# A new order for the second mixer's stage: loads, scores, page keys and page values of a hybrid decoder layer

## The chip, the cores and the metric

The kernel runs on one core of a Trainium2 chip. Its engines work side by side, each through its own list of instructions in order: TensorE (PE in the profile; PEld is its weight load), VectorE (DVE), ScalarE (ACT), GpSimd (POOL) and SyncE (SP), which here only starts transfers. They wait for each other by semaphores. The metric is the time of one execution on the device, in microseconds, as the median of several runs. One further execution is profiled; all views of the trace are of that one.

## The reference

One inference step of one decoder layer, for a prompt of 512 tokens and for 8 single sample tokens, which the kernel carries as N = 520 columns of a transposed activation. The layer adds two token mixers that work on the same normed input, merges them by sigmoid gates, and ends with a gated feed-forward part with a short convolution. Cut to the second mixer, forgetting attention with 8 heads of 128:

```python
q_f = rmsnorm(split_heads(fq, F_HEADS), f_qnorm_w)
k_f = rmsnorm(split_heads(fk, F_HEADS), f_knorm_w)
# prompt: causal, in blocks of 128 queries
s = einsum('bqhd,bkhd->bhqk', qi, k) * scale
s = s + (F_q - F_k)                  # F: running sum of log forget values
s = where(qpos >= kpos, s, -inf)
out = einsum('bhqk,bkhd->bqhd', softmax(s), v)
# sample: one new token over 2 pages of 128 cached keys and values, plus itself
pk = cache_k[layer, page_table]; pv = cache_v[layer, page_table]
merged = sigmoid(ga) * (y_m @ w_proj_a) + sigmoid(gb) * (y_f @ w_proj_b)
```

## The kernel before

Every large product is fp32, made of three products of rounded parts: a weight tile `raw` of 512 KB comes by a transfer of SyncE, ScalarE casts it to `wh` (L167), VectorE makes the rest `wl` (L168), and TensorE multiplies wh and wl with the two parts of the activation. Seven `raw` tiles and three pairs wh, wl exist at a time. A weight tile serves eight blocks of 128 rows; a block is six matmuls of 128x260, and `dense` takes one entry of the list `bg` behind each block. A block with its entry is called a step.

The stage of the second mixer is the last 12 column blocks of the input product (the gates of the merge), 16 steps each, so 192 steps. What runs beside them is written down in `plan`, a table from step to functions, which `put(step, function, ...)` fills. A head has 22 steps (`HP`), its base is b = 1 + 22 x head:

- `f_load` starts five transfers of 260 KB on SyncE: q, the row of inverse roots for q (spread over all partitions), k, the row for k, v. All five have the name `fi`.
- `f_norm` multiplies q and k by weight and row (L1534, two instructions of VectorE) and stores k (GpSimd's queue). `f_split` casts both on ScalarE (`fqh`, `fkh`) and makes the rests on GpSimd (`fql`, `fkl`). `f_forget` spreads the head's forget sums (`nFb`). `f_values` transposes v (`vtp`) and splits it.
- `f_scores(i)`, i from 0 to 3, makes the scores `fS` of a block of queries against all keys up to it, 128 to 512 wide, adds the forget sums and takes the maximum (VectorE L1566), the exponential (ScalarE L1568), and scales by the sum (VectorE L1570). The result is `fs`.
- `f_turn(j)` transposes the weights (`fPT`, L1581) and splits them (`fph`, `fpl`), `f_attend(j)` multiplies them with the values (`fy`), `y_split` splits the result.

The sample tokens run beside it. There are 16 pages of work, two halves of the heads by 8 tokens: `s_load` fetches a token's query row (`qb`, 256 KB, SyncE) and two tiles of cached keys (`kp`, gathers of GpSimd), `s_scores` multiplies and sums them on VectorE. These tiles come from a pool of nine, so three pages fit at a time. Behind the last, `s_bias`, `s_softmax` (transposes `sS`) and `s_weights` (transposes `sPT`, a memset of `pp` by GpSimd, a copy into it) make the weights; `s_gather` fetches 32 tiles of cached values (`vp`, GpSimd), `s_attend(n)` multiplies four of them (`sO`), and `s_heads` transposes each pair of results (`sOT`), which `ob` holds.

Ahead of the stage `run_pairs` works through pairs of column blocks; functions of the table `late_steps` run at its steps, seven to a pair: the inverse roots (`root_load`, `root_make`) and the sample rows (`rows_load`, `rows_make`) at the end. There the order of TensorE, VectorE and ScalarE is that of the program (class `Ordered`). In the stage itself the framework's scheduler orders the instructions of each engine, by the program's order and its own estimate of when operands are there; `plan` says only in which order they come to it.

## Time and profile before

| | |
|---|---|
| median of 3 runs | 2883.55 us (2879.86 to 2886.05) |
| profiled execution | 2878.56 us, span 2876.9 us, mean granted clock .995 |
| busy over the span | PE 2828.8 us (98%), DVE 2157.2 (75%), ACT 1360.1 (47%), POOL 409.3 (14%) |
| the stage | from 1004 to 1236 us |

A row of the timeline has the start in us, the duration, the engine, the line, the operation, output and inputs with their shapes, how many such instructions follow each other, and in brackets the idle time ahead of it and what ended it. A row of the waits has the line that waited, what released it, the total in us, how many times, and the longest. Numbers behind names of buffers are left out there.

### The profile page before, as it was taken

What the parts mean: (1) busy time and instruction counts of PE and PEld (TensorE: products, weight loads), DVE (VectorE), ACT (ScalarE), POOL (GpSimd) and SP (SyncE); (2) the same over time, 40 slices, a digit from 0 to 9 for tenths busy, and PEclk for the clock granted to TensorE, in tenths of its full rate; (3) what the DMA queues carried; (4) which work ended last, traced back from release to release, by engine and by line L of the source; (5) the groups of instructions that cost most, each with busy time, mean ns of one, the idle gap of its engine ahead of it and who ended that gap; (6) DMA issues with size and microseconds to landing.
All of it is one profiled execution on the core that took longest, in us unless ns stands there. A gap on an engine that the chain in (4) does not pass through costs nothing. (4 is left out here: it accounts for less than half of the span.)

```text
span 2876.9 us, 57590 instructions
## 1 busy us (share of the span) xinstructions
PE 2828.8 (98%) x23318; PEld 2715.0 (94%) x23318; DVE 2157.2 (75%) x3318; ACT 1360.1 (47%) x2131; POOL 409.3 (14%) x687
## 2 busy tenths in 40 slices
PE   8999999999999999899999999999999999999999
PEld 6888998999999989699999999999999999999999
DVE  5986755676767767568888887777787788787787
ACT  4335543455455544444555444444444445534543
POOL 0001111211101144501211010111110111100100
PEclk9999999999999999999999999999999999999999
DMA  9946658855555577566682444444444346745753
GB/s 339 311 145 205 216 184 274 278 177 195 180 178 191 179 240 232 196 214 219 206 266 85 129 134 142 144 147 144 143 132 130 115 151 181 213 149 170 191 159 104
DMA packets 226756, 531.44 MB, mean 185 GB/s; under 512 B 30305, under 2 KB 83025, under 8 KB 226489
## 3 DMA queue, kind: packets, MB, share of 16 engines
q1 hardware_dynamic: 187296, 426.89, 45.9%
q0 software_dynamic: 38752, 100.64, 11.5%
q8 instruction: 183, 3.00, 0.4%
q14 instruction: 85, 0.69, 0.1%
q10 hardware_dynamic: 440, 0.23, 0.0%
HBM read 451.28 MB, written 72.92 MB: 182 GB/s over the span
## 5 line engine op out<-in xcount | busy, mean ns | idle before, releaser
L60 DVE TENSOR_TENSOR wl<-raw,wh 128x1024 fp32r<-128x1024 f32 (+1 forms) x666 | 802.1, 1205 | 352.3 <-ACT wh L60 348.5
L60 ACT CAST wh<-raw 128x1024 fp32r<-128x1024 f32 (+1 forms) x666 | 689.4, 1036 | 757.2 <-DVE raw L60 389.1
L60 PE MATMUL x<-bf,wh 128*128 128x260 f32 x2624 | 475.8, 282 | 2.0 <-DVE tg L60 2.0
L60 DVE TENSOR_TENSOR raw<-raw,raw 128x1024 f32<-128x1024 f32 x339 | 413.9, 1221 | 5.8
L60 PEld LDWEIGHTS x<-bf,wh 128*128 128x128 f32 x2624 | 403.2, 188 | 2.2 <-ACT wh L60 2.2
L60 PE MATMUL x<-bf,wl 128*128 128x260 f32 x1312 | 369.7, 282 | 0.0
L60 PEld LDWEIGHTS x<-bf,wl 128*128 128x128 f32 x1312 | 246.8, 188 | 0.0
L60 PE MATMUL y<-bf,wh 128*128 128x260 f32 x1312 | 238.8, 282 | 0.0
L60 PEld LDWEIGHTS y<-bf,wh 128*128 128x128 f32 x1312 | 201.4, 188 | 0.0
L168 DVE TENSOR_TENSOR wl<-raw,wh 128x1024 fp32r<-128x1024 f32 x92 | 113.5, 1235 | 110.5 <-ACT wh L167 106.7
L60 PE MATMUL x<-ff,wh 128*128 128x260 f32 x1024 | 186.2, 283 | 0.0
L60 PE MATMUL x<-hf,wh 128*128 128x260 f32 x1008 | 185.5, 284 | 0.0
L60 PE MATMUL y<-bf,wl 128*128 128x260 f32 x656 | 184.7, 282 | 0.0
L167 ACT CAST wh<-raw 128x1024 fp32r<-128x1024 f32 x92 | 96.4, 1048 | 179.3 <-DMA raw<-in_w_in 40.7
L60 PEld LDWEIGHTS x<-hf,wh 128*128 128x128 f32 x1008 | 155.0, 188 | 13.4 <-issue 6.7
L60 PEld LDWEIGHTS x<-ff,wh 128*128 128x128 f32 x1024 | 157.6, 188 | 0.0
L60 PE MATMUL x<-ff,wl 128*128 128x260 f32 x512 | 144.5, 282 | 0.0
L60 PE MATMUL x<-hf,wl 128*128 128x260 f32 x504 | 142.3, 282 | 0.8 <-DVE wl L60 0.8
L60 PE MATMUL fo<-fe,wh 128*128 128x260 f32 x768 | 125.5, 284 | 1.1 <-DVE fo L60 0.9
L60 PEld LDWEIGHTS y<-bf,wl 128*128 128x128 f32 x656 | 123.7, 188 | 0.0
L60 PE MATMUL z<-bf,wh 128*128 128x260 f32 x656 | 120.6, 284 | 0.0
L60 PEld LDWEIGHTS fo<-fe,wh 128*128 128x128 f32 x768 | 105.8, 188 | 2.5 <-DVE fo L60 2.1
(640 smaller groups left out, 7077.9 us busy)
## 6 DMA issues: line engine op xcount, KB each, us to landing
raw<-in_w_fi SPq DMA_DIRECT2D x176, 512.0 KB
raw<-in_w_in SPq DMA_DIRECT2D x155, 512.0 KB
ar<-in_w_ada SPq DMA_DIRECT2D x192, 256.0 KB
raw<-in_w_ada SPq DMA_DIRECT2D x96, 512.0 KB
raw<-in_w_fo SPq DMA_DIRECT2D x64, 512.0 KB
raw<-in_w_out SPq DMA_DIRECT2D x32, 512.0 KB
raw<-in_w_fo SPq DMA_DIRECT2D x32, 384.0 KB
dff<-cc POOLq DMA_DIRECT2D x44, 260.0 KB
```

The costliest lines, as they stand in the source:

```text
L60: return lambda *a, **k: self.tc.keep_in_program_order(getattr(self.eng, op)(*a, **k))
L167: S.copy(wh[:, :n], raw[:, :n])
L168: V.tensor_tensor(wl[:, :n], raw[:, :n], wh[:, :n].bitcast(F32), op=ALU.subtract)
```

## The change

- `f_load`, `f_norm` and the list of heads are made ahead of `run_pairs`. Head 0's loads run in the last pair, 9 steps behind its start, when one operand of the pairs is given up (`hX.pop(5)`), and its norm 4 steps later, so both are ordered there as the pair's own work is. `rows_make` comes one step sooner.
- The other heads: loads at b - 18 instead of b - 12, `f_values` at b + 3 instead of b + 4 (and the tile of v is free behind it), scores at b + 8, 9, 11, 12 instead of 10, 11, 13, 15, turns as before at b + 20 to b + 22, `f_attend` from b + 26 instead of b + 25.
- Sample tokens: page loads at 6 + 7i instead of 2 + 8i, their scores at 18 + 7i instead of 14 + 8i. Softmax and weights 10 steps sooner (127 and 131), products of the values 8 steps sooner (from 137). The first eight gathers of values come at 126 to 133 instead of the first four at 135 to 138, each further group of four one to four steps behind a product, for the group two ahead (before: four to one steps ahead of a product, for the next group). `s_heads` seven steps behind its product instead of four.

```diff
--- before.py
+++ after.py
@@ -1428,6 +1428,25 @@
     root = {}
     dss, drr = dram([2, FH, N], "dss"), dram([2, FH, N], "drr")
 
+    def f_load(H):
+        H.q, H.k, H.rq, H.rk, H.v = (st("fi") for _ in range(5))
+        for t, src in ((H.q, dqk[0, H.i]), (H.rq, drr[0, H.i].partition_broadcast(P)), (H.k, dqk[1, H.i]),
+                       (H.rk, drr[1, H.i].partition_broadcast(P)), (H.v, dv[H.i])):
+            nc.sync.dma_start(t[:, :N], src)
+
+    def f_norm(H):
+        for t, w, r in ((H.q, qwc, H.rq), (H.k, nkw, H.rk)):
+            V.scalar_tensor_tensor(t[:, :N], t[:, :N], w, r[:, :N], op0=ALU.mult, op1=ALU.mult)
+        G.dma_start(O["kT"][:, H.i, :], H.k[:, :N])
+        H.rq = H.rk = None
+
+    heads = []
+    for hh in range(FH):
+        H = Head()
+        H.i, H.p, H.pt = hh, [], {}
+        heads.append(H)
+    H = None
+
     gates = list(range(NG, KC + NB2))
     others = [GatePair(gates[2 * i:2 * i + 2]) for i in range(len(gates) // 2)]
     others[1:1] = [ValuePair((2 * i, 2 * i + 1)) for i in range(FH // 2)]
@@ -1455,7 +1474,8 @@
         ada_store(SH2, late_ada.pop("sb"))
 
     t0 = 7 * (len(units) - 2)
-    late_steps = {7 * (KC + 2): late_turn, t0 + 1: root_load, t0 + 3: root_make, t0 + 6: rows_load, t0 + 9: rows_make}
+    late_steps = {7 * (KC + 2): late_turn, t0 + 1: root_load, t0 + 3: root_make, t0 + 6: rows_load, t0 + 8: rows_make,
+                  t0 + 9: lambda: (hX.pop(5), f_load(heads[0])), t0 + 13: on(f_norm, heads[0])}
     for k in range(KC):
         late_steps.update({7 * (1 + k) + 3: on(late_load, k), 7 * (1 + k) + 6: on(late_product, k)})
 
@@ -1523,18 +1543,6 @@
     yf = []
     log_exp()
 
-    def f_load(H):
-        H.q, H.k, H.rq, H.rk, H.v = (st("fi") for _ in range(5))
-        for t, src in ((H.q, dqk[0, H.i]), (H.rq, drr[0, H.i].partition_broadcast(P)), (H.k, dqk[1, H.i]),
-                       (H.rk, drr[1, H.i].partition_broadcast(P)), (H.v, dv[H.i])):
-            nc.sync.dma_start(t[:, :N], src)
-
-    def f_norm(H):
-        for t, w, r in ((H.q, qwc, H.rq), (H.k, nkw, H.rk)):
-            V.scalar_tensor_tensor(t[:, :N], t[:, :N], w, r[:, :N], op0=ALU.mult, op1=ALU.mult)
-        G.dma_start(O["kT"][:, H.i, :], H.k[:, :N])
-        H.rq = H.rk = None
-
     def f_split(H):
         H.qr = split(sp, "s", H.q, "fq", SEQ, G)
         H.kr = split(sp, "s", H.k, "fk", SEQ, G)
@@ -1547,6 +1555,7 @@
         H.vt = split(sp, "s", ps, "fv", 3 * P)
         H.last = st("last")
         S.copy(H.last[:, :P], ps[:, 3 * P:])
+        H.v = None
 
     def f_forget(H):
         psb = spread(R["nF"], H.i, "nFb")
@@ -1702,45 +1711,40 @@
         V.tensor_tensor(lo[:, SEQ:N], yS[:, :, hh], hi[:, SEQ:N].bitcast(F32), op=ALU.subtract)
 
     HP = 22
-    heads = []
-    for hh in range(FH):
-        H = Head()
-        H.i, H.p, H.pt = hh, [], {}
-        heads.append(H)
+    for hh, H in enumerate(heads):
         b = 1 + hh * HP
         if hh:
-            put(b - 12, f_load, H)
-        put(b, f_norm, H)
+            put(b - 18, f_load, H)
+            put(b, f_norm, H)
         put(b + 2, f_split, H)
         put(b + 1, f_forget, H)
-        put(b + 4, f_values, H)
-        for s, i in ((10, 0), (11, 1), (13, 2), (15, 3)):
+        put(b + 3, f_values, H)
+        for s, i in ((8, 0), (9, 1), (11, 2), (12, 3)):
             put(b + s, f_scores, H, i)
         for j in range(3):
             put(b + 20 + j, f_turn, H, j)
         for j in range(NB):
-            put(b + 25 + j, f_attend, H, j)
-        put(max(150 + 4 * hh, b + 30), y_split, hh)
-    f_load(heads[0])
+            put(b + 26 + j, f_attend, H, j)
+        put(max(148 + 4 * hh, b + 31), y_split, hh)
     for e in range(2):
         put(0, s_rows, e)
     for i in range(16):
-        put(8 * i + 2, s_load, i)
-        put(14 + 8 * i, s_scores, i)
-    put(136, s_bias)
-    put(137, s_softmax)
-    put(141, s_weights)
-    for i in range(4):
-        put(135 + i, s_gather, i)
+        put(6 + 7 * i, s_load, i)
+        put(18 + 7 * i, s_scores, i)
+    put(126, s_bias)
+    put(127, s_softmax)
+    put(131, s_weights)
+    for i in range(8):
+        put(126 + i, s_gather, i)
     for n in range(8):
-        t = 145 + 5 * n
+        t = 137 + 5 * n
         put(t, s_attend, n)
-        for i in range(n * 4 + 4, min(n * 4 + 8, 32)):
-            put(t - 4 + i % 4, s_gather, i)
+        for i in range(n * 4 + 8, min(n * 4 + 12, 32)):
+            put(t + 1 + i % 4, s_gather, i)
         if n % 2:
-            put(t + 4, s_heads, n // 2)
+            put(t + 7, s_heads, n // 2)
     for hh in range(FH):
-        put(185 if hh < FH - 1 else 187, y_sample, hh)
+        put(183 if hh < FH - 1 else 188, y_sample, hh)
 
     def run(fs):
         for f in fs:
```

How this moves instructions, at three places. First, head 0's softmax, while head 1's loads come. The order of SyncE there, before (`dqk` holds q and k, `drr` the rows of roots, `dv` the values, `dqf` the sample tokens' query rows):

```order
L1615 DMA qb1737_12150<-dqf1720_12094 128x512
L1615 DMA qb1751_12229<-dqf1720_12094 128x512
L1615 DMA qb1776_12353<-dqf1720_12094 128x512
L161 DMA raw1937_13196<-in_w_in 128x1024
L1530 DMA fi1757_12251<-dqk874_5549 128x520
L1530 DMA fi1759_12253<-drr878_5556 128x520
L1530 DMA fi1758_12252<-dqk874_5549 128x520
L1530 DMA fi1760_12254<-drr878_5556 128x520
```

and now:

```order
L1624 DMA qb1750_12203<-dqf1725_12107 128x512
L1435 DMA fi1745_12187<-dqk874_5549 128x520
L1435 DMA fi1747_12189<-drr878_5556 128x520
L1435 DMA fi1746_12188<-dqk874_5549 128x520
L1435 DMA fi1748_12190<-drr878_5556 128x520
L161 DMA raw1946_13226<-in_w_in 128x1024
L1435 DMA fi1749_12191<-dv872_5548 128x520
L1624 DMA qb1768_12303<-dqf1725_12107 128x512
```

Two of the three first query rows went from ahead of head 1's loads to behind them. VectorE, from the maximum of head 0's last scores (the ISA row with `fS`) to their scaling by the sum, before:

```order
L1566 ISA fs1774_12334,sm1775_12335<-fS1773_12329,nfb1736_12148 128x512
L1566 ISA sm1775_12335 128x1
L1570 TENSOR_SCALAR fs1763_12272<-fs1763_12272,sm1764_12273 128x256
L1569 RECIPROCAL sm1767_12297<-sm1767_12297 128x1
L1567 TENSOR_SCALAR sm1775_12335<-sm1775_12335 128x1
L1534 SCALAR_TENSOR_TENSOR fi1758_12252<-fi1758_12252,nkw_5552,fi1760_12254 128x520
L1570 TENSOR_SCALAR fs1766_12296<-fs1766_12296,sm1767_12297 128x384
L60 TENSOR_TENSOR kp1738_12152<-kp1738_12152,qb1737_12150 128x512
L1569 RECIPROCAL sm1775_12335<-sm1775_12335 128x1
L60 TENSOR_REDUCE sc_12095<-kp1738_12152 128x4
L60 TENSOR_TENSOR kp1739_12153<-kp1739_12153,qb1737_12150 128x512
L1570 TENSOR_SCALAR fs1774_12334<-fs1774_12334,sm1775_12335 128x512
```

and now:

```order
L1575 ISA fs1766_12296,sm1767_12297<-fS1765_12291,nfb1736_12148 128x512
L1575 ISA sm1767_12297 128x1
L1578 RECIPROCAL sm1764_12279<-sm1764_12279 128x1
L1439 SCALAR_TENSOR_TENSOR fi1746_12188<-fi1746_12188,nkw_5552,fi1748_12190 128x520
L1579 TENSOR_SCALAR fs1763_12278<-fs1763_12278,sm1764_12279 128x384
L168 TENSOR_TENSOR wl1818_12545<-raw1816_12542,wh1817_12544 128x1024
L1576 TENSOR_SCALAR sm1767_12297<-sm1767_12297 128x1
L60 TENSOR_TENSOR kp1769_12305<-kp1769_12305,qb1768_12303 128x512
L60 TENSOR_REDUCE sc_12108<-kp1769_12305 128x4
L1578 RECIPROCAL sm1767_12297<-sm1767_12297 128x1
L60 TENSOR_TENSOR kp1770_12306<-kp1770_12306,qb1768_12303 128x512
L1579 TENSOR_SCALAR fs1766_12296<-fs1766_12296,sm1767_12297 128x512
```

The page that is multiplied there was the first (its query row is the first that SyncE fetched) and is now the second, whose query row stands last in SyncE's rows above; a weight row `wl` is there as well. TensorE took the transposes of head 0's first three `fs`, then the fourth behind 12 gate matmuls; now it takes the four one behind the other.

Second, head 4's softmax on VectorE, before, from three rows behind the maximum of the last scores to their scaling:

```order
L1569 RECIPROCAL sm1994_13485<-sm1994_13485 128x1
L1567 TENSOR_SCALAR sm2003_13543<-sm2003_13543 128x1
L1534 SCALAR_TENSOR_TENSOR fi1987_13463<-fi1987_13463,qwc_5550,fi1989_13465 128x520
L1570 TENSOR_SCALAR fs1993_13484<-fs1993_13484,sm1994_13485 128x256
L1569 RECIPROCAL sm1997_13509<-sm1997_13509 128x1
L1534 SCALAR_TENSOR_TENSOR fi1988_13464<-fi1988_13464,nkw_5552,fi1990_13466 128x520
L1570 TENSOR_SCALAR fs1996_13508<-fs1996_13508,sm1997_13509 128x384
L60 TENSOR_TENSOR kp1964_13343<-kp1964_13343,qb1963_13341 128x512
L1569 RECIPROCAL sm2003_13543<-sm2003_13543 128x1
L60 TENSOR_REDUCE sc_12095<-kp1964_13343 128x4
L60 TENSOR_TENSOR kp1965_13344<-kp1965_13344,qb1963_13341 128x512
L1570 TENSOR_SCALAR fs2002_13542<-fs2002_13542,sm2003_13543 128x512
```

and now, from that maximum itself:

```order
L1575 ISA fs2002_13524,sm2003_13525<-fS2001_13519,nfb1965_13349 128x512
L1575 ISA sm2003_13525 128x1
L1578 RECIPROCAL sm2000_13507<-sm2000_13507 128x1
L1576 TENSOR_SCALAR sm2003_13525<-sm2003_13525 128x1
L1579 TENSOR_SCALAR fs1999_13506<-fs1999_13506,sm2000_13507 128x384
L1578 RECIPROCAL sm2003_13525<-sm2003_13525 128x1
L1579 TENSOR_SCALAR fs2002_13524<-fs2002_13524,sm2003_13525 128x512
```

The norm of head 5 and a page of keys stood in it and no longer do.

Third, GpSimd at the first group of cached values, before (`fql` and `fkl` are head 6's):

```order
L225 TENSOR_TENSOR fql2076_13950<-fi2042_13762,fqh2075_13949 128x512
L225 TENSOR_TENSOR fkl2078_13954<-fi2043_13763,fkh2077_13953 128x512
L868 DMA vp2079_13957<-in_cache_v,idx0_2452 128x512
L868 DMA vp2084_13976<-in_cache_v,idx0_2452 128x512
L868 DMA vp2092_14010<-in_cache_v,idx0_2452 128x512
L868 DMA vp2093_14021<-in_cache_v,idx0_2452 128x512
L1654 MEMSET pp1721_12096 128x512
L868 DMA vp2120_14148<-in_cache_v,idx1_2456 128x512
```

and now (`dsg` is a store of a gate):

```order
L868 DMA vp2059_13853<-in_cache_v,idx0_2452 128x512
L868 DMA vp2063_13873<-in_cache_v,idx0_2452 128x512
L868 DMA vp2069_13891<-in_cache_v,idx0_2452 128x512
L1767 DMA dsg870_5547<-sgm2064_13875 128x520
L868 DMA vp2070_13899<-in_cache_v,idx0_2452 128x512
L1663 MEMSET pp1726_12109 128x512
L225 TENSOR_TENSOR fql2088_13986<-fi2038_13707,fqh2087_13985 128x512
L225 TENSOR_TENSOR fkl2090_13990<-fi2039_13708,fkh2089_13989 128x512
```

The first group (`vp` with `idx0`, four rows) and the memset of the weights went from behind head 6's pair to ahead of it; four more gathers, the second group, stand ahead of these rows. At the last head's pair 17 of the 32 gathers stood ahead of it and 15 behind; now 24 and 8.

## The prediction

> **What bounds the kernel now.** I began with the page's busy times, and then asked only for the stage that the change touches, since elsewhere the order of the work is the same.
>
> ```profile
> PE 2828.8 (98%) x23318; PEld 2715.0 (94%) x23318; DVE 2157.2 (75%) x3318; ACT 1360.1 (47%) x2131; POOL 409.3 (14%) x687
> ```
>
> TensorE (PE) is busy 98% of the span, so time can only come from its idle stretches and from stretches in which its clock is lower. The second mixer's stage runs from 1004 to 1236 us. The waits of TensorE from 985 to 1240 (total, times, longest):
>
> ```profile
> PE fPT L1581 <- DVE fs L1570: 7.7, 6, 2.3
> PE sO L1673 <- DMA vp<-in_cache_v,idx: 3.1, 1, 3.1
> PE sO L1673 <- issue: 2.5, 2, 1.4
> PE sOT L1684 <- ACT ob L1677: 1.8, 1, 1.8
> PE fS L1194 <- POOL fkl L225: 1.4, 1, 1.4
> PE gate L213 <- issue: 1.3, 2, 0.8
> PE x L60 <- DVE wl L60: 0.8, 1, 0.8
> ```
>
> They sum to 18.6 us. The second price is the clock. In the table of stretches (length, PE, PEld, DVE, ACT and POOL busy, granted clock, DMA share, GB/s) five rows matter:
>
> ```profile
> 1004.00:1027.00 23.00, 21.49 (x171) 20.39 (x169) 7.63 (x22) 9.94 (x19) 11.92 (x13) 1.00 0.83 281
> 1027.00:1036.00 9.00, 6.64 (x33) 6.42 (x34) 6.96 (x16) 3.62 (x8) 2.55 (x3) 0.62 0.62 200
> 1126.00:1132.00 6.00, 5.29 (x31) 5.19 (x32) 5.33 (x10) 2.20 (x4) 2.17 (x3) 0.72 0.43 141
> 1164.00:1176.00 12.00, 7.76 (x42) 4.95 (x40) 4.28 (x17) 1.68 (x5) 8.70 (x11) 0.86 0.88 301
> 1198.00:1222.00 24.00, 19.52 (x128) 13.80 (x123) 10.68 (x38) 8.59 (x22) 12.01 (x12) 0.93 0.62 186
> ```
>
> What the clock cost, as length times one minus clock: 9 x .38 = 3.4, 6 x .28 = 1.7, 12 x .14 = 1.7, 24 x .07 = 1.7 us, together 8.5. So the most that a better order can bring is 18.6 + 8.5 = 27 us, 0.9%. The change adds and removes no instruction and no byte; every term below is one of these waits.
>
> **Last pair, the first head's norm (0.8 us).** The wait at x L60 is one wl of VectorE (DVE) that stood behind the first head's norm. That norm now stands behind the last pair's wl rows, and the square roots' rows come one step earlier. I take -0.8; bounds -0.8 and +0.8 (the same wait again, elsewhere).
>
> **Head 0's turn.** TensorE and then VectorE there:
>
> ```profile
> 1027.81 0.33 PE L1581 MATMUL fPT<-ident,fs 128*128 128x128 f32 x1 [2.32 <-DVE fs L1570]
> 1029.69 0.48 PE L1581 MATMUL fPT<-ident,fs 128*128 128x128 f32 x1 [1.54 <-DVE fs L1570]
> ```
>
> ```profile
> 1024.86 0.76 DVE L1534 SCALAR_TENSOR_TENSOR fi<-fi,qwc,fi 128x520 f32<-128x520 f32 x1 [4.37 <-DMA fi<-drr]
> 1028.54 0.76 DVE L1534 SCALAR_TENSOR_TENSOR fi<-fi,nkw,fi 128x520 f32<-128x520 f32 x1 [0.66 <-DMA fi<-drr]
> 1029.21 0.41 DVE L1570 TENSOR_SCALAR fs<-fs,sm 128x384 f32<-128x384 f32 x1
> 1029.55 0.68 DVE L60 TENSOR_TENSOR kp<-kp,qb 128x512 f32<-128x512 f32 x1
> 1030.26 0.69 DVE L60 TENSOR_REDUCE sc<-kp 128x4 f32<-128x512 f32 x1
> 1031.46 0.48 DVE L1570 TENSOR_SCALAR fs<-fs,sm 128x512 f32<-128x512 f32 x1
> ```
>
> Head 1's norm sits inside head 0's softmax and waits for its loads; the scalings fs and TensorE's transposes fPT are late behind it: 3.86 us. These loads were issued here by SyncE (SP), with the sizes from the view of the transfers:
>
> ```profile
> 1012.64 1.84 SPq L1615 DMA_DIRECT2D qb<-dqf  x3
> 1015.20 0.33 SPq L161 DMA_DIRECT2D raw<-in_w_in  x1
> 1015.62 0.38 SPq L1530 DMA_DIRECT2D fi<-dqk  x1
> 1017.07 1.10 SPq L1530 DMA_DIRECT2D fi<-drr  x1
> ```
>
> ```profile
> raw<-in_w_in SPq DMA_DIRECT2D x4, 512.0 KB
> qb<-dqf SPq DMA_DIRECT2D x4, 256.0 KB
> fi<-dqk SPq DMA_DIRECT2D x2, 260.0 KB
> ```
>
> In the change the four fi come right behind the first qb, some 2.4 us sooner, since SyncE still waits for the rows that qb reads. Ahead of head 1's second root row (the last that its norm needs) SyncE's queue held .77 (three qb) + .52 (raw) + 1.04 MB = 2.33 MB, landed at 1028.5. Now the first norm needs .78 MB and the second 1.30. By the same pace (2.33 MB in 15.9 us) that is some 5.3 and 8.9 us after 1012.6: about 1018 and 1021.5. So the norm is no longer what is late. Late next is sample token 1's query row qb: it stands behind the first qb, four fi, raw and v, and the queue up to its own end holds 2.34 MB again, so it lands at about 1028. The order of VectorE puts both page-key multiplications of that token ahead of the fourth scaling. From 1028: .68 + .69 + .16 + .68 + .48 (the rows above) = 2.7, so fs is ready at 1030.7. TensorE now transposes all four fs in one run, before any gate product, and reaches them at about 1025.2 - .8 + .4 (three transposes) = 1024.8. It would stand still some 5.9 us: +2.0 against the 3.86 of before. Behind the waiting row stand the fpl of the turn and one wl of the next gate but one, which is wanted 8 steps later; behind TensorE's transposes stands everything of TensorE. Bounds: qb there in time, when VectorE gets to it at about 1025.5, gives 1028.2 and so 3.5, -0.4; landing 2 us later, +3.8. The lower clock (3.4) stays.
>
> A rule of the Trainium skill bears on the queue: "DMA: Bandwidth & Descriptors", section "Issuing engines are not separate DMA queues", says that transfers started by SyncE and by GpSimd run on the same 16 engines and interleave. The trace agrees: the 1004 to 1027 stretch is at a DMA share of .83 with six page-key gathers in it. By it an earlier issue alone brings nothing here, which would leave this head as it was, term 0 instead of +2.0 and a sum of -13.9.
>
> **Heads 1 to 6, the turns.** Of the 7.7 us, 3.86 are head 0's; the other 3.84 are heads 1, 2, 4 and 6. Head 4 has the largest:
>
> ```profile
> 1125.57 0.76 DVE L1534 SCALAR_TENSOR_TENSOR fi<-fi,nkw,fi 128x520 f32<-128x520 f32 x1 [2.20 <-DMA fi<-drr]
> 1126.71 0.58 PE L1581 MATMUL fPT<-ident,fs 128*128 128x128 f32 x3 [2.21 <-DVE fs L1570]
> ```
>
> The change puts loads 6 steps sooner and the last scores 3 steps sooner, so 8 gate steps instead of 5 lie between the last scores and the first turn. A step is six matmuls of .126 us (21.49 us for 171 in the first row of stretches), .75 us, so 2.3 us more than before stand behind each score. In head 4 neither a norm nor a page key stands between last scores and last scaling any more; in heads 1 and 2 four or five page-key rows do, .7 us each, and VectorE then ends about when TensorE arrives. I leave .8 us of waiting there, and take the lower clock at 1126 (1.7) as gone: -3.0 - 1.7 = -4.7. Bounds -5.5 and -1.
>
> The Trainium skill speaks otherwise of that clock: "TensorE: Matmul & The Clock Gate", section "HAM oscillation — how this bites in real kernels", puts the abstract rule at idle gaps above some 3.4 us. The row above has 2.21 us idle and a clock of .72 behind it, so the measurement decides; by the page the 1.7 would not hang on this wait, and the sum would be -10.2.
>
> **fkl (1.4 us).** Scores two steps sooner want GpSimd's fkl about 1.5 us sooner. Against it, a page-key gather (.95 busy, .30 between) no longer stands between fql and fkl for heads 2 and 3, and head 2's turns end earlier, so that head 3's chain starts earlier. I take -1.0; bounds -1.4 and +1.5.
>
> **Start of the page values.**
>
> ```profile
> 1164.34 1.64 POOL L868 DMA_INDIRECT vp<-in_cache_v,idx  x1 [0.30 <-issue]
> 1165.97 0.54 POOL L1654 MEMSET pp<- 128x512 f32 x1
> 1166.94 1.06 PE L1673 MATMUL sO<-vp,pp 128*32 128x512 f32 x6 [1.14 <-issue]
> 1171.10 1.58 PE L1673 MATMUL sO<-vp,pp 128*32 128x512 f32 x2 [3.10 <-DMA vp<-in_cache_v,idx]
> ```
>
> The first group's fourth gather was issued 6.8 us before its product, and the memset that the weights need stood behind it: the whole group stood behind head 6's fql and fkl on GpSimd. Now eight gathers and the memset stand ahead of that pair, and 6 steps instead of 4 lie between weights and product. The gathers bring the same bytes, so what covers them is the gate work of head 5, whose cover is needed for some 5 us of issue (four times .95 + .30) and the landing. All of it is 1.14 + 3.10 + 1.7 = 5.9; I take -5.4, bounds -5.9 and -2 (the fourth gather still behind head 6's v at the memory).
>
> **The last head.**
>
> ```profile
> 1188.49 1.29 POOL L225 TENSOR_TENSOR fql<-fi,fqh 128x512 fp32r<-128x512 f32 x1 [4.59 <-ACT fqh L224]
> 1191.63 1.77 POOL L868 DMA_INDIRECT vp<-in_cache_v,idx  x1 [0.15 <-issue]
> 1211.58 0.95 POOL L868 DMA_INDIRECT vp<-in_cache_v,idx  x1 [0.30 <-issue]
> ```
>
> GpSimd waits 4.59 us for fql and then issues 15 gathers in one row to 1212.5, beside which fall 1.35 (sO), 1.3 (gate), 1.79 (sOT) and 1.7 of clock, 6.1 in all. Now 24 of the 32 gathers stand ahead of fql, 8 behind it, and the heads' transposes sOT come three steps later. I take -4.6; bounds -6.1 and +2 (the eight still late).
>
> **New waits.** The sample scores' transposes sS now stand right ahead of head 5's turn, 63 gate matmuls behind the last scores, and the weights' transposes only 12 gate and 4 transpose matmuls behind sS. The softmax between took
>
> ```profile
> 1159.96 0.42 DVE L1641 TENSOR_REDUCE smx<-sS 64x1 f32<-64x257 f32 x1 [0.71 <-PE sS L1639]
> 1162.01 0.35 DVE L1645 TENSOR_SCALAR pp<-pp,smx 64x257 f32<-64x257 f32 x1
> ```
>
> 2.4 us, and those 16 matmuls give about 2: +0.6, bounds 0 and +3. Page keys every 7 steps instead of 8 make DMA, GpSimd and VectorE denser: a page is two multiplications and two sums, 3.0 us of VectorE by
>
> ```profile
> L60 DVE TENSOR_TENSOR kp<-kp,qb 128x512 f32<-128x512 f32 x32 | 26.2, 819 | 0.0
> ```
>
> (and .68 a sum), so a head's 22 steps hold 3.1 pages instead of 2.75, 1.2 us more of VectorE to a head. What collides there no row shows. I put +2 for it, bounds 0 and +5 (one more wait like 1171's with its clock).
>
> **Sum.** -0.8 + 2.0 - 4.7 - 1.0 - 5.4 - 4.6 + 0.6 + 2.0 = -11.9. The profiled execution took 2878.56 (span 2876.9), 5 below the median of the three runs; -11.9 from it gives 2866.7, and from the median 2883.55 **2871.6 us**.
>
> **Rivals.**
> - The whole of it: every wait goes but head 0's, as the terms' best bounds say (-0.8 - 0.4 - 5.5 - 1.4 - 5.9 - 6.1 = -20.1): 2863.4. For it speaks the slack of 2.3 us a head and of eight gathers; against it that VectorE is not idle for long in any softmax, and that the same bytes now fall into fewer steps.
> - The waits only move: heads 1 to 6 keep theirs, because the scheduler again puts norms and page keys into each softmax, and the last eight gathers are late. Then only the start of the page values is gained, and head 0 is lost: -5.4 + 2.0 + 0.6 = -2.8: 2880.7. It is also what the change not doing its work would look like.
> - Slower: VectorE's row of page keys. If, as at head 0, a multiplication that waits for its qb or kp stands ahead of the last scaling, TensorE stands 2.7 us or more and loses 1.7 of clock. At four more heads that is 4 x 4.4 = 17.6, and with the other terms 17.6 + 2.0 - 0.8 - 5.4 - 4.6 = +8.8: 2892.4. It decides from the point where a page's loads land later than the last scores. For it: the denser pages. Against it: the kp row above has 0.0 idle before all its 32 multiplications, and three pages fit into the buffers at a time.
>
> **Chances.** Forecast (-6 to -17) .54, the whole .13, moved .20, slower .13. Changes below 0.2% (5.8 us) can't be told from none. Faster .67 (.53 of the forecast, the whole, .01 of moved), same .19, slower .14. The forecast's own range is 2867 to 2878; with the others 8 in 10 lie in **2861 to 2885**.
>
> **What would show it.** Right: head 0's fPT waits 4 to 7 us behind a kp row that waits for qb; no fPT wait above 1 us in heads 1 to 6, clock 1.00 around head 4; no sO wait for vp at the start; fewer than 2 us idle in the last 35 us. Wrong: sPT or sS waits above 2 us, kp rows of VectorE that wait for DMA at later heads, or the vp wait again at a later group.

## The result and the profile after

The changed kernel takes 2863.05 us (median of five runs, 2862.7 to 2864.11) against 2879.94 us of the kernel before (2875.71 to 2886.05): ratio 0.9938, 95% interval 0.9924 to 0.9953. It is faster, by 17 us (0.6%) where 12 were forecast. Its profiled execution took 2862.7 us (span 2861.0) against 2878.56, a difference of 15.9 us, and the forecast for it was 2866.7.

TensorE's waits from 985 to 1240 us in the changed kernel (columns as before: total, times, longest):

```profile
PE fPT L1590 <- DVE fs L1579: 5.2, 4, 3.2
PE vtp L1554 <- PE nFb L400: 0.4, 1, 0.4
PE sO L1682 <- DMA vp<-in_cache_v,idx: 0.4, 1, 0.4
PE sPT L1659 <- DVE pp L1654: 0.3, 1, 0.3
PE sO L1682 <- issue: 0.2, 1, 0.2
```

18.6 us of waits have become 6.5, and 4.8 of these 6.5 are head 0's turn. The stretches (length, busy times, granted clock, DMA share, GB/s):

```profile
1022.00:1036.00 14.00, 9.18 (x53) 8.46 (x53) 11.10 (x32) 6.70 (x15) 5.56 (x6) 0.78 0.91 322
1108.00:1130.00 22.00, 22.00 (x178) 21.31 (x177) 19.79 (x42) 10.47 (x23) 11.28 (x13) 1.00 0.76 245
1150.00:1164.00 14.00, 13.26 (x91) 9.38 (x90) 4.30 (x12) 5.12 (x12) 8.06 (x8) 1.00 0.71 244
1186.00:1208.00 22.00, 21.81 (x162) 17.02 (x162) 11.75 (x43) 10.54 (x25) 9.50 (x10) 1.00 0.53 181
```

Of the four stretches of lower clock one is left: 14 x .22 = 3.1 us of some 8.5 (3.4 us with what runs past 1036). One loss shows in no wait. The products sO come in eight groups of eight. Four of the groups take 1.06 us each; three others, in which next to no wait is booked, took 3.07, 2.20 and 2.9 us, in TensorE's timeline:

```profile
1170.71 3.07 PE L1682 MATMUL sO<-vp,pp 128*32 128x512 f32 x8
1178.84 2.20 PE L1682 MATMUL sO<-vp,pp 128*32 128x512 f32 x8
...
1194.48 1.05 PE L1682 MATMUL sO<-vp,pp 128*32 128x512 f32 x4
1195.72 1.69 PE L1682 MATMUL sO<-vp,pp 128*32 128x512 f32 x4 [0.19 <-issue]
1197.34 0.50 PE L213 MATMUL gate<-hh,wh 128*128 128x260 f32 x2
```

The last of these ran at a third of its pace, 1.8 us lost with next to nothing booked as idle. Over all eight groups, what is beyond 1.06 us each, booked waits left out, sums to 5.9 us here and to 3.5 us in the kernel before.

At head 0 VectorE shows this (its timeline, the rows that matter):

```profile
1018.27 0.69 DVE L60 TENSOR_TENSOR kp<-kp,qb 128x512 f32<-128x512 f32 x1 [3.39 <-DMA kp<-in_cache_k,idx]
...
1021.75 0.69 DVE L60 TENSOR_TENSOR kp<-kp,qb 128x512 f32<-128x512 f32 x1 [2.06 <-DMA kp<-in_cache_k,idx]
...
1025.47 0.68 DVE L1575 CUSTOM_DVE_ANT_0 fs<-fS,nfb 128x512 f32<-128x512 f32 x1
...
1026.15 0.74 DVE L1439 SCALAR_TENSOR_TENSOR fi<-fi,nkw,fi 128x520 f32<-128x520 f32 x1
...
1027.14 1.22 DVE L168 TENSOR_TENSOR wl<-raw,wh 128x1024 fp32r<-128x1024 f32 x1
1028.27 0.15 DVE L1576 TENSOR_SCALAR sm<-sm 128x1 f32<-128x1 f32 x1
1028.34 0.68 DVE L60 TENSOR_TENSOR kp<-kp,qb 128x512 f32<-128x512 f32 x1
...
1030.32 0.48 DVE L1579 TENSOR_SCALAR fs<-fs,sm 128x512 f32<-128x512 f32 x1
```

The rows of page 0 stand ahead of the whole softmax and wait 3.39 and 2.06 us for gathers. The row of page 1 at 1028.34 waits for nothing: its query row qb was there. The last maximum starts at 1025.47. Behind it stand the second half of head 1's norm, a scaling and a weight row, then the small row at 1028.27 that the last exponential waits for, then page 1's rows, none of them with a wait. The last scaling is ready at 1030.8, as forecast, but what made it late is not what was forecast.

### The profile page after: what moved, and what is told of

Same layout as the page of the kernel before. It is cut to its first block, busy times and chain, and to the rows that moved or that the text cites. A ratio compares the mean times of both kernels' runs of the same rounds, so it can differ in the third digit from the quotient of the medians.

```text
span 2861.0 us, 57607 instructions
## 1 busy us (share of the span) xinstructions
PE 2825.4 (99%) x23318; PEld 2711.8 (95%) x23318; DVE 2154.0 (75%) x3318; ACT 1360.5 (48%) x2131; POOL 413.3 (14%) x687
## 4 chain that ended last, share of the span: by engine, by line
PE 85%; DVE 5%; issue 5%; DMA 2%; ACT 2%; POOL 1%; SPq 0%; POOLq 0%; DVEq 0%; ACTq 0%
PE x L60 33%; PE y L60 17%; PE z L60 8%; PE gate L213 4%; PE pre L60 3%; PE fo L60 3%; PE pa L213 3%; PE mo L213 2%; PE adp L60 2%; PE mv L213 2%; PE adp L409 1%; DVE wl L60 1%; PE mq L213 1%; PE mk L213 1%; ACT wh L60 1%
## 5 line engine op out<-in xcount | busy, mean ns | idle before, releaser
L60 ACT CAST wh<-raw 128x1024 fp32r<-128x1024 f32 (+1 forms) x666 | 689.5, 1036 | 754.7 <-DVE raw L60 386.3
```

The lines of the kernel that those rows point to most:

```text
L60: return lambda *a, **k: self.tc.keep_in_program_order(getattr(self.eng, op)(*a, **k))
```

## The experiments

Twelve runs in three groups; the kernels of one group ran side by side, on one chip, with the kernel before, whose median was 2873.6, 2879.1 and 2873.9 us in them; each group had another chip. That spread is larger than many of the effects, so the table has three measures: the time, the ratio to the kernel before in its own group, and, from the profiled execution, the length of the stage (from the first product of sbias to the last row of gate products) with TensorE's stops in it in three places. A kernel has one profile, so a stop of a microsecond or two in one row can be that execution's alone.

| kernel | us | ratio, 95% interval | stage, us | head 0 | heads 1 to 6 | page values and last head |
|---|---|---|---|---|---|---|
| before | 2879.94 | | 230.1 | 3.9 | 5.3 | 8.6 |
| the change | 2863.05 | .9938 (.9924 to .9953) | 215.2 | 4.8 | .4 | 1.2 |
| e1, pages 0, 1 at 24, 29 | 2857.49 | .9947 (.9930 to .9964) | 210.8 | 3.8 | .4 | 1.4 |
| e2, pages 0, 1 at 22, 27 | 2864.53 | .9973 (.9962 to .9983) | 213.5 | 1.6 | 5.4 | 1.2 |
| e3, heads alone | 2864.11 | .9971 (.9960 to .9982) | 214.3 | 2.0 | 7.5 | .5 |
| e4, sample tokens alone | 2883.60 | 1.0035 (1.0021 to 1.0049) | 234.1 | 5.3 | 10.1 | 4.5 |
| e5, loads alone | 2874.25 | .9982 (.9972 to .9991) | 224.7 | 3.6 | 2.0 | 7.8 |
| e6, scores alone | 2877.59 | .9997 (.9987 to 1.0007) | 229.6 | 3.3 | 7.5 | 7.3 |
| e7, the change again | 2860.53 | .9934 (.9918 to .9951) | 212.7 | 4.9 | .8 | 1.0 |
| e8, pages 0, 1 at 26, 31 | 2857.47 | .9928 (.9911 to .9945) | 209.6 | 2.4 | 1.7 | 1.3 |
| e9, loads and scores | 2864.87 | .9969 (.9959 to .9980) | 217.4 | 2.8 | 6.3 | 1.1 |
| e10, heads again | 2862.23 | .9956 (.9942 to .9970) | 216.5 | 2.0 | 6.1 | 1.9 |
| e11, heads and page keys | 2859.45 | .9952 (.9936 to .9969) | 210.2 | 4.9 | .4 | 1.2 |
| e12, as e8, norms later | 2855.12 | .9932 (.9915 to .9948) | 209.1 | 2.1 | 1.2 | 1.3 |

e1 to e4 are one group, e5 to e8 and e9 to e12 the others.

### What holds head 0: pages 0 and 1 later

```diff
-        put(18 + 7 * i, s_scores, i)
+        put(18 + 7 * i if i > 1 else 24 + 5 * i, s_scores, i)   # e1; e2: 22 + 5 * i
```

> The changed kernel with the scores of pages 0 and 1 planned at steps 24 and 29 instead of 18 and 25. VectorE's order still has page 0's key rows ahead of head 0's softmax, but page 1's no longer stand between its last maximum and its last scaling. Theory Q (the prediction's: page 1's query row and rows are what holds the last scaling): head 0's fPT waits fall from 4.8 to under 1 us and the lower clock there goes, 4 + 3 = about -7 against the changed kernel, so 0.991 to 0.992 of before. Theory G (the trace's: VectorE stands 5.4 us for page 0's key gathers, and everything of head 0 is late behind it): the last maximum still comes at 1025.5; scaling, weight row, exponential follow, the last scaling is ready at about 1029.5 to 1029.8, the waits are still 3.5 to 4 us and the clock stays low: -1, 0.9935.

> The changed kernel with the scores of pages 0 and 1 planned at steps 22 and 27. In VectorE's order both pages' key rows now stand behind head 0's softmax. Theory G: VectorE no longer waits for the gathers; head 0's fPT waits fall from 4.8 to at most 1 us and the lower clock of 1030 to 1036 goes: 4 + 3 = -7, 2856, 0.9914 of before; 6 us faster than the kernel that moves page 1 alone. Theory Q: the same as that kernel within 1 us. A third possibility: the norm's own loads are as late as the gathers (both share the DMA engines), then VectorE waits for fi<-drr to 1021 or 1022 instead and the gain is 2 us or less in both.

In e1 head 0's stops fell only from 4.8 to 3.8 us, and VectorE still waited 3.62 and .98 us for gathers of page 0 ahead of the softmax: the query row qb is not the holder. With page 0's scores put two steps earlier, in e2, they came behind the softmax, the stops there fell to 1.6 us and the clock of the stretch 1022 to 1036 was 1.00 instead of .78. But 3.2 us of stop came up at head 2, where head 3's norm rows now waited for their loads. Over all e2 gained nothing against e1, and its time is the longer one by 7 us. The order that VectorE gets is thus not that of the step numbers: page 0 at 22 fell behind the softmax, at 24 ahead of it. No run holds e1 beside the change: by ratio it is not the faster one (.9947 against .9938), by stage it is.

e8 moves both pages further:

```diff
-        put(18 + 7 * i, s_scores, i)
+        put(18 + 7 * i if i > 1 else 26 + 5 * i, s_scores, i)
```

> The changed kernel with the key rows of pages 0 and 1 at steps 26 and 31 instead of 18 and 25: both stand behind head 0's softmax, and page 1 behind the start of head 1's. Theory G (page 0's gathers, landing 5 to 9 us behind their issue, hold head 0's last scaling): the stops at head 0 fall from 4.8 to 2 us or less, and if nothing takes their place the time is 3 to 4 us below the change's (2.8 us of waits and up to 1.5 us of clock). Rival (as with both pages at 22 and 27): the next load in VectorE's order, head 1's norm rows, takes the place, the stops only move to heads 1 or 2, and the time is within 1.5 us of the change's.

VectorE at head 0 in e8:

```profile
1019.96 0.76 DVE L1439 SCALAR_TENSOR_TENSOR fi<-fi,qwc,fi 128x520 f32<-128x520 f32 x1 [5.24 <-DMA fi<-drr]
1023.33 0.76 DVE L1439 SCALAR_TENSOR_TENSOR fi<-fi,nkw,fi 128x520 f32<-128x520 f32 x1 [1.45 <-DMA fi<-drr]
```

The waiting moved from page 0's gathers to head 1's norm, as the rival said, but the stops fell to 2.4 us, clock 1.00. The wait itself did not get shorter: VectorE stands 6.7 us here and 5.5 in the change, and the last maximum starts only .6 us sooner, counted from the start of the stage (20.6 against 21.2 us). But from that maximum to the end of the last scaling it takes 5.3 us in the change, 4.5 in e1 and 3.1 in e2 and e8, where no page row stands between and the row that the last exponential waits for follows the maximum closely. So of the 2.8 us by which the last scaling comes sooner in e8, 2.2 are rows behind the maximum that waited for nothing. Beside e7 in the same group e8 is 3.1 us shorter by the medians, and its stage 3.1 us; the runs of the two overlap (2856.4 to 2863.0 and 2859.3 to 2862.3), so the gain is probable and not certain.

### The two halves of the change

e3 has the edits to the heads and every step of the sample tokens as before; e10 is the same kernel in another group. e4 has the sample tokens' steps alone.

```diff
 # e3, e10: the change with the sample tokens' steps of before
-        put(6 + 7 * i, s_load, i)
-        put(18 + 7 * i, s_scores, i)
+        put(8 * i + 2, s_load, i)
+        put(14 + 8 * i, s_scores, i)
 ...      # and s_bias to y_sample as before; e4: before with the change's numbers there
```

> The changed kernel with all of the sample tokens' steps (pages, softmax, weights, gathers, products) set back to those of before: last pair, heads' loads, scores and turns alone. If the terms of the sum are independent: -0.8 (last pair), -5.2 (turns of heads 1 to 6 with the clock), -1.4 (fkl) = -7, with head 0 at -1 to +1: 0.9975 of before, and the waits for vp, sO, sOT of before remain at 8 us or so. If the halves only work together (pages as before collide with the earlier scores): under 3 us gained, 0.999 or more.

> The kernel before with the sample tokens' steps of the change alone: pages every 7 steps, values earlier, gathers two groups ahead, head transposes later. Independent terms: -5.5 (start of the page values) and -5.9 (last head) with the fPT waits of before: -11, 0.996. If denser pages cost the softmaxes something that the earlier scores pay for: fPT waits of 10 us or more instead of 7.7 with another stretch of low clock, -6 or less, 0.998.

> The change's edits to the heads with every sample-token step as before (e3's kernel), timed again beside the runs of this group, since the kernel before spread from 2871 to 2883 us between groups and e3 and the whole change were not timed side by side. 2861 to 2866 us, ratio 0.9945 to 0.998. If the next run is within 1.5 us of it, the earlier page keys are worth nothing by themselves.

TensorE's waits in e3, then in e4:

```profile
PE fPT L1590 <- DVE fs L1579: 7.9, 6, 3.2
PE fS L1194 <- DVE sm L1575: 1.7, 1, 1.7
PE sPT L1659 <- DVE sm L1576: 0.5, 1, 0.5
```

```profile
PE fPT L1581 <- DVE fs L1570: 15.0, 7, 4.9
PE sO L1673 <- DMA vp<-in_cache_v,idx: 4.5, 3, 3.6
```

The heads' half gave 9 to 12 us by the medians of its two groups, and not where I had expected them: the stops at the page values and the last head are gone (8.6 to .5 and 1.9), with the gathers' steps as before, while those at the heads' turns stayed. The sample half alone made the kernel 10 us slower. It does what I had forecast of the gathers at two places: its first two groups of products do not wait, and no stop above .5 us is left at the last head. But the third group now waits:

```profile
1181.92 2.72 PE L1673 MATMUL sO<-vp,pp 128*32 128x512 f32 x6 [3.60 <-DMA vp<-in_cache_v,idx]
```

VectorE in e4:

```profile
1023.61 0.69 DVE L60 TENSOR_TENSOR kp<-kp,qb 128x512 f32<-128x512 f32 x1 [8.41 <-DMA kp<-in_cache_k,idx]
1076.95 0.69 DVE L60 TENSOR_TENSOR kp<-kp,qb 128x512 f32<-128x512 f32 x1 [4.51 <-DMA kp<-in_cache_k,idx]
```

and TensorE behind the second of them:

```profile
1083.16 0.47 PE L1581 MATMUL fPT<-ident,fs 128*128 128x128 f32 x1 [4.94 <-DVE fs L1570]
```

So a page-key row that waits for its gather inside the softmax does hold TensorE: the stop that follows it is 4.9 us. Norm rows and further page rows stand between the two as well.

### Within the heads' half: loads and scores

```diff
-            put(b - 12, f_load, H)
+            put(b - 18, f_load, H)                                # e5, e9
-        for s, i in ((10, 0), (11, 1), (13, 2), (15, 3)):
+        for s, i in ((8, 0), (9, 1), (11, 2), (12, 3)):           # e6, e9
```

> The kernel before with one change: each head's loads 18 steps ahead instead of 12. With the scores, turns, first head and page steps as before. Theory L (the loads set both ends): head 7's loads then leave SyncE's queue some 10 us earlier (about 1154 instead of 1165.6), clear of the first page-value gathers (1160.6 to 1166.0), so the three stops at the start of the page values (3.1 + 1.1 + 1.7 us before) fall under 1 us, and the earlier-landing q and k rows take half or more of the stops at fPT of heads 1 to 6: TensorE's waits sum to about 10 instead of 18.6 us and the time is 8 us below before, ratio about 0.997. Theory S (the earlier scores give the slack): the page-value stops go, but the fPT stops stay at 9 to 10 us, ratio about 0.9985. If the time doesn't fall at all, or rises as the whole page half did (e4, +10 us), earlier loads alone crowd the page-key gathers, and neither holds.

> The kernel before with one change: a head's four score steps 8, 9, 11 and 12 steps behind its start instead of 10, 11, 13 and 15. Theory S: each softmax then starts some 2 to 3 steps earlier while the turn stays where it was, so the fPT stops of heads 1 to 6 fall from 4.6 to under 1 us, with them the clock loss behind the 2.2 us idle, and the time falls by 4 to 6 us, ratio about 0.998; the page-value stops of 5.9 us stay, since head 7's loads stand where they stood. Theory L: the scores themselves wait for the loads (VectorE's fi row and the norm), so TensorE's stops move from fPT to sS or fS and the time stays within 1.5 us of before.

> The kernel before with two edits together: each head's loads 18 steps ahead and its four score steps at 8, 9, 11 and 12. All else as before. Alone, the loads gave ratio 0.9982 and the scores 0.9997; all edits to the heads together 0.9971 (some 8 us), with no stop at the page values. Theory A (the two edits need each other: a score step can only come earlier if its rows are there): the two together give what the whole heads' half gave, ratio 0.997, fPT waits of heads 1 to 6 below 2.5 us, and no stop of TensorE at 1206 to 1214. Theory B (the rest of the heads' half does it: the first head in the last pair, the attend steps one later): the stops of 4 to 5 us near 1207 to 1214 stay, and the ratio is 0.998, as with the loads alone.

The loads alone gave 5 us, the scores alone nothing that can be measured, both together 9 us, by the medians of their groups; the intervals of e9 and e3 are nearly the same. So the loads and the scores are the heads' half; what else it has (the first head in the last pair, products one step later) adds 2.6 us in e10 beside e9, with intervals that overlap. By place each expectation failed in part. Earlier loads alone took the turns of heads 1 to 6 from 5.3 to 2.0 us, and the first page values no longer wait, both as theory L had it:

```profile
1167.66 1.07 PE L1673 MATMUL sO<-vp,pp 128*32 128x512 f32 x8
...
1182.60 1.24 PE L1673 MATMUL sO<-vp,pp 128*32 128x512 f32 x8 [3.20 <-DVE fpl L225]
```

Nearly all of the 7.8 us that the table has for e5 are elsewhere: 4.1 at head 6's last turn (the second row, and two short stops ahead of it) and 3.5 at the last head. Earlier scores alone took the turns to 7.5; there too the first page values don't wait, against theory S, and the 7.3 us are 2.6 behind head 6's last turn and 4.7 at the last head. The two together cleared the last head as well, with the turns at 6.3, where theory A had put them below 2.5.

What e9 does settle is the gathers. TensorE's waits and the ends of GpSimd's row of 15 gathers in e9:

```profile
PE fPT L1581 <- DVE fs L1570: 9.1, 5, 3.2
PE x L60 <- DVE wl L60: 2.0, 1, 2.0
PE sPT L1650 <- DVE pp L1645: 1.1, 1, 1.1
```

```profile
1186.07 1.75 POOL L225 TENSOR_TENSOR fkl<-fi,fkh 128x512 fp32r<-128x512 f32 x1
1187.98 1.77 POOL L868 DMA_INDIRECT vp<-in_cache_v,idx  x1 [0.15 <-issue]
...
1206.98 0.96 POOL L868 DMA_INDIRECT vp<-in_cache_v,idx  x1 [0.30 <-PE gate L213]
```

Fifteen gathers still stand in one row behind the last head's fkl, and no product of the page values waits (the first eight only ran slower, 2.51 us instead of 1.06). The gathers' order alone is not what stopped the kernel before. With e4 it follows that at the last head either half alone clears the stops, and at the first page values every edit that was tried did.

### The page keys and the page values

e11 is the change with the values' steps as before:

```diff
-    put(126, s_bias)
-    put(127, s_softmax)
-    put(131, s_weights)
-    for i in range(8):
-        put(126 + i, s_gather, i)
+    put(136, s_bias)
+    put(137, s_softmax)
+    put(141, s_weights)
+    for i in range(4):
+        put(135 + i, s_gather, i)
 ...      # products, gathers, s_heads and y_sample likewise
```

> The change with the page values' steps (bias, softmax, gathers, attends, heads and outputs of the sample tokens) as before; the page keys' loads and scores and all edits to the heads as in the change. My prediction put 5.4 us at the start of the page values and 4.6 us at the last head down to the gathers' order. If that holds, both stops come back here: 8 to 10 us more than the change, about 2871 us. If the edits to the heads alone removed them, as the heads' half suggests, no vp wait above 1 us is left and the time is within 2 us of the change's 2860.5 to 2863 us.

```profile
PE fPT L1590 <- DVE fs L1579: 5.3, 4, 3.2
PE sPT L1659 <- DVE sm L1576: 1.2, 1, 1.2
```

```profile
1177.78 1.77 POOL L868 DMA_INDIRECT vp<-in_cache_v,idx  x1
...
1197.57 0.95 POOL L868 DMA_INDIRECT vp<-in_cache_v,idx  x1 [0.30 <-issue]
```

Neither stop comes back: 2859.45 us, no longer than the change. That comparison is across groups. By ratio e11 (.9952) lies behind the change (.9938 and .9934), with intervals that overlap; by stage it is 2.5 to 5 us ahead, about what the products sO lose there beyond their 1.06 us: .6 us in e11, 5.9 and 3.1 in the two profiles of the change. So the runs show no gain of the page values' new steps beside the heads' edits, and can't exclude one. The page keys' new steps on top of the heads' half probably do gain: e11's median is 2.8 us below e10's in the same group, but the runs overlap (2858.7 to 2861.1 and 2858.8 to 2865.0). Its stage is 6.3 us shorter (e10's profile is of its slowest run), and in the trace the stops of heads 1 to 6 go from 6.1 to .4 us, while head 0's rise from 2.0 to 4.9. VectorE in e10 at head 2:

```profile
1064.04 0.76 DVE L1439 SCALAR_TENSOR_TENSOR fi<-fi,qwc,fi 128x520 f32<-128x520 f32 x1 [3.21 <-DMA fi<-drr]
1067.50 0.76 DVE L1439 SCALAR_TENSOR_TENSOR fi<-fi,nkw,fi 128x520 f32<-128x520 f32 x1 [1.91 <-DMA fi<-drr]
```

These are head 3's norm rows amid head 2's softmax. In e11 the first of them waits 5.56 us but ahead of the whole softmax, and the second not at all. Head 0 of e11 also shows what I had forecast for the change and what it did not do: a page-key row waits for its query row,

```profile
DVE kp L60 <- DMA qb<-dqf: 3.5, 1, 3.5
DVE kp L60 <- DMA kp<-in_cache_k,idx: 2.0, 1, 2.0
```

but page 0's, not page 1's, and TensorE's 4.9 us there are the change's own.

### The change again, and the norms later

> The changed kernel itself, on the same chip as the runs beside it, so that the two halves and the later page keys can be held against it: ratio 0.994 as first measured, with 0.9924 to 0.9964 allowed. If e1's 0.9947 was this ratio too, the later page keys gained nothing over the change; if this run shows 0.996 to 0.997 here, they gained some 4 us.

e7 is the changed kernel, unedited: .9934, and its stage 2.5 us shorter than in the first profile, as much as the products sO lose less (3.1 us instead of 5.9; the last slow group above took 1.06 us here).

```diff
-            put(b, f_norm, H)
+            put(b + 1, f_norm, H)                                 # with pages 0, 1 at 26, 31
```

> The changed kernel with the key rows of pages 0 and 1 at steps 26 and 31 and each head's norm one step later (b + 1 instead of b), behind the last turn step of the head ahead of it. In the run with the pages at 26 and 31, head 1's norm stood in head 0's softmax on VectorE and waited 5.2 and 1.5 us for its loads, and head 4's norm (1.5 us) stood right ahead of the last scaling, with a stop of 1.5 us behind it. Theory N (the norms are the next holder): VectorE's norm rows come behind the last scaling, the stops at head 0 fall from 2.4 us to under 1 and the one of head 4 goes: 2854 to 2856 us. Rival: the scheduler orders by when it thinks rows are ready and puts them where they were, and the time stays at 2857.5.

e12 has the lowest time of all, 2855.12 us (2851.73 to 2856.36). Its profile does not bear out the reason: head 1's norm rows stand amid head 0's softmax as in e8 and wait 4.96 and 1.49 us. Only the stop behind head 4's norm, at head 3's turn, fell, from 1.47 to .93. By ratio (.9932, .9915 to .9948) it can't be told from e8 or the change; by its stage, 209.1 us, it is level with e8 and 3.7 to 6.1 us ahead of the change. Whoever goes on starts from e12, with a gain over the change of some 3 to 6 us that still wants a direct comparison.

## Why the prediction was right, and where it was not

Sign and size hold: 2863.05 lies in the range, and the gain, 16.9 us by the medians, is at the edge of the forecast's own 6 to 17. As a time it lies outside the forecast's own 2867 to 2878 and on the rival "the whole of it" (2863.4), which had .13; and what that rival says, that every wait goes but head 0's, is what the waits above show to within 1.7 us. Of the 8.5 us between forecast and result, 4 are the sum's. The rest is the base: I added to a median of 2883.55 that came from three runs, while the changed kernel runs within 1.4 us of its profiled time.

By terms, waits and clock from the first profile after against those of before:

| term | forecast | measured |
|---|---|---|
| last pair | -0.8 | -0.8 |
| head 0 | +2.0 | +1.0 |
| heads 1 to 6 | -4.7 | -3.5 and -1.7 of clock, -5.2 |
| fkl | -1.0 | -1.4 |
| start of page values | -5.4 | -5.5 |
| last head | -4.6 | -6.1, and +1.8 of slow sO and .2 of wait, -4.1 |
| new waits | +0.6 | +0.7 |
| collisions | +2.0 | nothing found |
| sum | -11.9 | -15.3 (profiled times: -15.9) |

The last head's row counts only its own slow sO; over all groups they are 2.4 us more than before. The largest mis-sized term is the collisions of denser page keys: 2 us put for something no row showed, and e11, which has the denser keys, stops TensorE for .4 us at heads 1 to 6. Right sizes do not make right steps, though:

- **Head 0.** The end came out to a tenth of a microsecond, 1030.8 against 1030.7, through the wrong holder. The step that failed is that VectorE waits for page 1's query row. The landing itself was not far off: the change's profile has no time for it, but in e11, whose plan is the same up to step 126, that row was issued at 1015.97 and landed at 1026.89, .9 us before VectorE came to it. What was wrong is when VectorE comes: at about 1025.5 by the forecast, so that with the row there in time the scaling is ready at 1028.2. At 1025.47 VectorE only began the last maximum, and it came to page 1 at 1028.34. Two things that I had left out make up the difference. Page 0's rows waited ahead of the softmax, for gathers that GpSimd issued at 1012.6 and 1013.95 and that VectorE got at 1018.27 and 1021.75; I had passed them over, since they waited for nothing before. And norm, scaling and weight row stand between the maximum and page 1; I had the order, and did not add them up. e2 and e8, in which both pages go behind the softmax, bring the stop to 1.6 and 2.4 us; e1, in which only page 1 does, to 3.8. The queue rule of the Trainium skill ("DMA: Bandwidth & Descriptors", "Issuing engines are not separate DMA queues") gave 0 for this term; with +1.0 measured, the runs lie halfway and decide nothing on it. The gathers that came 5.7 and 7.8 us behind their issue beside SyncE's loads agree with it.
- **Heads 1 to 6.** I credited the loads and scores. They do not do it: e9, e3 and e10, which have both, stand 6.1 to 7.5 us there, more than the 5.3 of before. It takes the page keys' steps as well (e11: .4). What the scores gain in slack a norm row that waits in the softmax takes again.
- **Start of the page values, and the last head.** Both sizes were right, and the cause I gave is not the only one. I had read "15 gathers in one row behind fql" as the reason. With the new order of the gathers alone (e4) both stops do go, and 3.6 us come up at the third group. But e3, e9, e10 and e11 keep that row of 15 and have no stop either. At the last head the loads and scores of the heads, which I had put to the turns, are enough, and only both together: e5 and e6 still stop there for 3.5 and 4.7 us. At the first page values the loads alone are enough, and so are the scores alone: a wait of more than .6 us there stands in the profile of the kernel before and in no other. Which edit removed the stops in the change can't be told, since either half does; why the heads' edits do is open (below).
- **The slower rival** had .13. Its mechanism is real: the sample half without the heads' half is 10 us slower, with the very rows it named, kp that wait for a gather in the softmax and 4.9 us of TensorE. Its point of decision, page loads later than the last scores, is met there and not in the whole change, in which such a row waits only at head 0.
- **The clock.** The stretch around head 4 is at 1.00 now that its 2.2 us stop is gone, and the 1.7 us came back, as the measured row had it. Whether a stop of that size costs anything depends on where it falls (below), so the term hung on one execution. By the idle gap of some 3.4 us that the Trainium skill names ("TensorE: Matmul & The Clock Gate", "HAM oscillation — how this bites in real kernels") they would have stayed lost. Head 0's loss is 3.4 us before and after.

## What to carry to other kernels

A wait names the last thing that was late, and not what made room for it: undo one part at a time before crediting a gain to the edit that stands nearest to the wait. On an engine that works in order, add up every row between the one that you follow and its goal, also those that wait for nothing: at head 0 taking them out halved the stop, while the wait ahead of the softmax stayed. And two parts of a reordering need not add: here -9 to -12 and +10 us made -17. If either of two edits removes a stop, taking one of them back shows nothing: each has to be tried alone as well.

## What the runs showed of the hardware

In the kernel before and in e5 three engines stop at once beside a row of gathers, and the trace names no instruction as the reason; in e6 ScalarE and TensorE do. ScalarE and TensorE in e5:

```profile
1206.37 0.61 ACT L224 CAST yfh<-yf 128x512 fp32r<-128x512 f32 x1
1212.76 0.59 ACT L1677 COPY ob<-sO 128x512 f32<-128x512 f32 x1 [5.78 <-remote]
```

```profile
1208.31 0.28 PE L213 MATMUL gate<-hh,wl 128*128 128x260 f32 x1 [1.01 <-issue]
1209.73 0.28 PE L213 MATMUL gate<-hl,wh 128*128 128x260 f32 x1 [0.78 <-issue]
1211.86 0.38 PE L213 MATMUL gate<-hh,wh 128*128 128x260 f32 x1 [1.48 <-issue]
```

The copy's input was done at 1205.8. GpSimd's last gather was issued from 1209.89 to 1210.85, and VectorE came back at 1212.59. ScalarE has another such stop in e5 (4.77 us, to 1181.23), ahead of the cast that fpl waits for, and with it the product at 1182.60. e7 and e8 have one of ScalarE as well (4.88 us, to 1195.87, e7's last gather at 1193.62; 4.76 us in e8), behind which TensorE did not stop. e3 and e9 to e12 have rows of gathers and no such stop. What the engines wait for, and why the stops come and go with the order of the other work, the runs do not show.

The clock after a stop was not a matter of the stop's length alone. Two stops of 1.34 and 3.25 us gave .78 in the stretch 1022 to 1036 (the change), 1.35 and 2.43 (e1) .76, .54 and 1.59 (e12) .88, .78 and 1.59 (e8) 1.00: the last two differ by a quarter of a microsecond the other way. The granted clock itself is either 1.00 or .50 in these traces, and the stretches above are means of the two. In the stage every loss lasts 3.41 us or twice that, and in each profile all losses start a whole number of 3.41 us apart. Two such periods each of the kernel before and of e12 (columns as for the stretches):

```profile
1123.70:1127.11 3.41, 1.20 (x11) 0.99 (x10) 1.54 (x3) 0.00 (x0) 0.48 (x1) 1.00 0.56 221
1127.11:1130.53 3.42, 3.42 (x17) 3.32 (x16) 3.11 (x7) 1.05 (x1) 1.06 (x2) 0.50 0.41 151
```

```profile
1024.14:1027.55 3.41, 1.68 (x13) 1.50 (x14) 2.23 (x5) 2.03 (x5) 0.56 (x1) 1.00 0.84 258
1027.55:1030.96 3.41, 3.41 (x18) 3.31 (x17) 2.13 (x4) 1.96 (x4) 0.00 (x0) 0.50 0.58 189
```

Cut into such periods, the 14 profiles agree from 985 to 1240 us: each of the 28 periods at full clock in which TensorE stood still for 1.73 us or more was followed by one at .50, and none of the 983 with 1.65 us or less was. In e8 a boundary at 1026.84 cuts the second stop in two and leaves 1.3 and 1.0 us to the two periods, so nothing was lost. The periods lie differently in each execution, so by this the same stop can cost 1.7 us of clock in one and nothing in another. Outside the stage idle time alone does not decide: around 1470 to 1495 us 1.1 to 1.6 us were enough in eight profiles, and around 1568 1.8 us were not in two.
